# A 2 KB load as the first DMA of a row-maximum kernel, with the first 8 MB load behind the opening barrier

## The chip, the cores and the metric

The kernel runs on one core of a Trainium2 chip. The metric is the device time in microseconds (us); several runs give a median. A separate execution was recorded by the hardware profiler, and what is said below of the inside of a run comes from that one.

## The reference

For each of the 8192 rows of an fp32 matrix with 8192 columns, the largest absolute value:

```python
def reference(x):
    return np.linalg.norm(x, ord=np.inf, axis=1)
```

Every byte of the 268 MB input must be read once, and 8192 numbers are written.

## The kernel before

Each of the 128 SBUF partitions takes 64 rows: 38 "bulk" rows, 24 "tail" rows and 2 rows of the very first load. The first load (`x_f`, line 241) and the 19 bulk loads are of the same shape: 2 rows of 8192 values in each partition, 64 KB a partition and 8 MB in all. They go in turn into the three slots of one SBUF ring (lines 264 to 269). VectorE reduces each with one instruction, `absmax` (line 256), to two numbers per partition. The tail is 34 loads whose widths shrink toward the end (the table `TAIL`, loaded in line 303), so that little work is left when the last bytes land. Their reductions partly write a partial maximum into the ring just ahead of the next piece of the same row, so that the next reduction takes it in.

All loads are issued from SyncE (SP), in the order of the program, on one hardware DMA queue. A load into a used slot waits for the reduction that read the slot last. Loads rotate over eight completion semaphores, `DMAHW0` to `DMAHW7`; VectorE waits for the load's own semaphore. Two stores of results go out from ScalarE's queue near the end (lines 328 and 330), and a last one of 2 KB from SP (line 332).

Four edits are made on the finished instruction lists. What matters here:

- `start_first_load_early` (line 32) takes the first DMA that SP issues and puts it ahead of everything that SP does in the opening block. That block holds a barrier: each of SP, ScalarE and TensorE signals GpSimd, GpSimd answers with a release, and only then does an engine go on to the body. So the first DMA is issued before the barrier, and all others come behind it. In the code above the change, the first DMA is the 8 MB load of `x_f`.
- `finish_on_pool` (line 71) makes GpSimd wait for the last stores and clear the semaphores. The semaphore of the last store is left out of the clearing, since it is awaited last; what lies below it and above it is cleared by one instruction each, if there is anything there (lines 108 to 110).
- `drop_implied_waits` (line 132) removes waits that other waits imply. `open_without_vector` (line 184) takes VectorE out of the opening barrier.

`SPARE` unused semaphores are allocated ahead of the others (line 243), which sets the numbers that the others get. A tile `gap` rounds the small tiles to a multiple of 128 values, so that the ring starts at a fixed place (lines 250 to 253).

Of the kernel before, what the change touches and what calls it, by code (L numbers as in the profile page):

```python
# [12 lines left out]
F32 = mybir.dt.float32  # L13
# [4 lines left out]
HEAD, STEP = 32, 8  # L18
# [191 lines left out]
def kernel(  # L210
# [4 lines left out]
    B: int = 2,  # L215
    SLOTS: int = 3,
    PAD: int = 128,
    SPARE: int = 12,
):
    nc = tc.nc  # L220
    P = nc.NUM_PARTITIONS
# [11 lines left out]
    n_bulk_rows = rows // P - n_tail - B  # L233
# [7 lines left out]
    x_f = x_t[:, n_tail * cols :]  # L241
# [3 lines left out]
    pool = ctx.enter_context(tc.tile_pool(name="sbuf", bufs=1))  # L245
    r_bulk = pool.tile([P, n_bulk_rows], F32)
    n_soon = n_tail - 2
    r_soon = pool.tile([P, n_soon], F32)
    r_late = pool.tile([P, 2 + B], F32)
    used = [HEAD, n_bulk_rows, n_soon, 2 + B]  # L250
    gap = -sum(-(-n // STEP) * STEP for n in used) % PAD
    pool.tile([P, gap], F32, name="gap")
    ring = pool.tile([P, R], F32)
# [1 line left out]
    def absmax(o, i):  # L255
        return nc.vector.reduce_max(  # L256
            out=o, in_=i, axis=X, apply_absolute_value=True
        )

    def after(ins, first, kind):  # L260
        info = mybir.DependencyInfo(kind, mybir.DependencyReason.SCHED_ONLY)
        tc.add_manual_dep(ins.ins, first.ins.name, info, reason="order")

    for n in range(N):
        at = n % SLOTS * W
        t = ring[:, at : at + W]
        nc.sync.dma_start(out=t, in_=x_f if n == 0 else x_b[n - 1])
        r = r_late[:, 2:] if n == 0 else r_bulk[:, (n - 1) * B : n * B]
        absmax(r, t.rearrange("p (b c) -> p b c", b=B))
# [97 lines left out]
```

## Time and profile before

| | us |
|---|---|
| median of 3 runs | 626.26 (626.0 to 626.3) |
| the profiled execution's own time | 626.09 |
| its span, first to last instruction | 623.5 |
| VectorE busy | 552.3 (89% of the span) |
| bytes read from HBM | 268.44 MB, 431 GB/s over the span |

The span begins when SP issues the first DMA. The profiled execution's time is 2.6 us longer than its span: it also counts something ahead of the first instruction and, behind the last one shown, the landing of the last store. In the rows of the profile, `SPq` is SP's queue of instructions, among them the DMA issues. A DMA is issued by one instruction of some 0.3 us, is carried out by 16 DMA engines as packets of up to 64 KB, and lands later. In a table by windows the last two columns are the DMA share, which is the time of all packets that begin in the window as a share of 16 engines, and GB/s, which are their bytes. Both count a packet in the window in which it begins; so in a short window the share may be over 1, and the number of packets and their mean duration can be worked out.

### The profile page before, as it was taken

To read this page: it belongs to the slowest core of one execution; us is meant where nothing else is said; L and a number is where in the kernel's file an instruction comes from. 1 tells how busy PE (TensorE), PEld (TensorE's weight loads), DVE (VectorE), ACT (ScalarE), POOL (GpSimd) and SP (SyncE) were. 2 spreads that over 40 slices of the span, in tenths; PEclk is the share of its full clock that TensorE was granted. 3 is DMA by queue.
4 is the path that set the end of the run, shared out by engine and by line. 5 is a ranking of instruction groups with operands and counts; after the bars stand their busy time and mean duration, and the time that the engine had idled before them with its cause. 6 is when DMAs were issued, how large, how long until landed. Compare 5 with 4: busy or idle time off the path is not lost.

```text
span 623.5 us, 152 instructions
## 1 busy us (share of the span) xinstructions
DVE 552.3 (89%) x64; POOL 0.2 (0%) x4
## 2 busy tenths in 40 slices
DVE  0588988889988899888898888988889999999999
POOL 0000000000000000000000000000000000000000
DMA  9999999999999999999999999999999999999998
GB/s 404 471 404 446 429 408 467 404 471 404 471 404 467 408 441 433 408 467 404 471 404 471 404 467 408 441 433 408 467 428 435 415 437 419 447 422 431 428 425 357
DMA packets 8065, 268.48 MB, mean 431 GB/s; under 512 B 1152, under 2 KB 1152, under 8 KB 2560
## 3 DMA queue, kind: packets, MB, share of 16 engines
q1 hardware_dynamic: 7776, 268.44, 99.7%
q10 hardware_dynamic: 288, 0.03, 0.0%
q14 instruction: 1, 0.01, 0.0%
HBM read 268.44 MB, written 0.03 MB: 431 GB/s over the span
## 4 chain that ended last, share of the span: by engine, by line
DMA 65%; DVE 35%; another core or an unknown queue 0%; issue 0%; DVEq 0%
DMA ring<-in_x_dram 65%; DVE r_bulk L256 19%; DVE r_soon L256 14%; DVE ring L256 1%; DVEq L362 0%; DVE r_late L256 0%
## 5 line engine op out<-in xcount | busy, mean ns | idle before, releaser
L256 DVE TENSOR_REDUCE r_bulk<-ring 128x2 f32<-128x16384 f32 x19 | 327.2, 17220 | 40.0 <-DMA ring<-in_x_dram 40.0
L256 DVE TENSOR_REDUCE r_soon<-ring 128x1 f32<-128x8192 f32 (+9 forms) x18 | 148.0, 8249 | 8.4 <-DMA ring<-in_x_dram 8.4
L256 DVE TENSOR_REDUCE ring<-ring 128x1 f32<-128x4992 f32 (+23 forms) x24 | 59.7, 2539 | 0.1
L256 DVE TENSOR_REDUCE r_late<-ring 128x2 f32<-128x16384 f32 (+2 forms) x3 | 18.9, 6329 | 21.9 <-DMA ring<-in_x_dram 21.9
L351 POOL MEMSET const-bfloat16-1.0<- 128x1 bf16 x1 | 0.1, 101 | 0.0
L351 POOL MEMSET const-uint8-127<- 128x1 uint8 x1 | 0.1, 101 | 0.0
L351 POOL MEMSET const-float32-0.0<- 128x1 f32 x1 | 0.1, 98 | 0.2 <-issue 0.2
L351 POOL MEMSET const-float32-1.0<- 128x1 f32 x1 | 0.1, 98 | 0.0
## 6 DMA issues: line engine op xcount, KB each, us to landing
ring<-in_x_dram SPq DMA_DIRECT2D x3, 4096.0 KB, 30.7
ring<-in_x_dram SPq DMA_DIRECT2D x2, 3744.0 KB, 38.6
ring<-in_x_dram SPq DMA_DIRECT2D x1, 6592.0 KB, 37.0
ring<-in_x_dram SPq DMA_DIRECT2D x1, 5696.0 KB, 31.1
ring<-in_x_dram SPq DMA_DIRECT2D x1, 4480.0 KB, 37.5
ring<-in_x_dram SPq DMA_DIRECT2D x1, 3328.0 KB, 42.5
ring<-in_x_dram SPq DMA_DIRECT2D x1, 2912.0 KB, 40.8
ring<-in_x_dram SPq DMA_DIRECT2D x1, 2592.0 KB, 38.3
```

Source lines behind the costliest of these rows:

```text
L256: return nc.vector.reduce_max(out=o, in_=i, axis=X, apply_absolute_value=True)
L351: nc = _bacc.Bacc("TRN2", target_bir_lowering=False, num_devices=1)
```

## The change

A tile `opener` of 128 x 16 values is added. Ahead of the loop, SP issues a load of 16 values (64 bytes) into each fourth partition of it, from the first 64 bytes of the rows that the first 8 MB load brings for these partitions: 32 runs of 64 bytes, 2 KB. Nothing reads the tile. Since the load is now the first DMA that SP issues, `start_first_load_early` moves it, and no longer the 8 MB load, ahead of the barrier.

```diff
-    SPARE: int = 12,
+    SPARE: int = 11,
+    OPEN: int = 16,
...
+    opener = pool.tile([P, OPEN], F32)
-    used = [HEAD, n_bulk_rows, n_soon, 2 + B]
+    used = [HEAD, n_bulk_rows, n_soon, 2 + B, OPEN]
...
+    nc.sync.dma_start(out=opener[::4, :], in_=x_f[::4, :OPEN])
     for n in range(N):
         at = n % SLOTS * W
```

In the built program SP's list begins with the opener, then come the barrier and the 20 loads of 8 MB. The load of each place takes the semaphore of the next lane (the first 8 MB load `DMAHW1` in place of `DMAHW0`), so the eighth 8 MB load also waits for the lane that the opener used. The semaphore of the last store is no longer the lowest of its range, and GpSimd clears the range with two instructions in place of one. The order of the instructions of VectorE, ScalarE and TensorE is the same, and the ring starts at the same place: the opener's 16 values come out of `gap`.

## The prediction

> **What bounds the kernel now.** I read the page first, for what is busy, then tables by windows, for how evenly.
>
> ```profile
> span 623.5 us, 152 instructions
> ...
> DVE 552.3 (89%) x64; POOL 0.2 (0%) x4
> ...
> q1 hardware_dynamic: 7776, 268.44, 99.7%
> ```
>
> VectorE is idle for 11% of the span. The one queue of loads fills the 16 DMA engines for 99.7%. The next view asks whether there is a gap anywhere in the middle (window, its length, VectorE and GpSimd busy, clock, DMA share, GB/s):
>
> ```profile
> 5.00:105.00 100.00, 74.68 (x5) 0.00 (x0) 1.00 0.99 430
> 105.00:205.00 100.00, 89.51 (x6) 0.00 (x0) 1.00 1.01 440
> ...
> 505.00:605.00 100.00, 99.88 (x26) 0.00 (x0) 1.00 1.00 431
> 605.00:621.00 16.00, 16.00 (x11) 0.00 (x0) 1.00 1.01 419
> ```
>
> There is none: the share stays at 0.99 to 1.01 from 5 us until the last bytes. So every DMA engine runs packet behind packet, and it ends when it started in earnest plus a fixed amount of work. The time can move at only two places: how soon the engines run at full rate, and what follows the last landing. The change touches the first.
>
> For the first 5 us I read SP's own instructions (the first rows for the first load alone, the next for the barrier in SP's queue, then the second load), and then narrow windows.
>
> ```profile
> L267 SPq DMA_DIRECT2D ring<-in_x_dram x1: 362/362/362, 0.0 to 0.0; - x1
> ...
> DMA to landing us min/median/max: 21.8/21.8/21.8
> ```
> ```profile
> L351 SPq DRAIN  x1: 131/131/131, 0.4 to 0.4; - x1
> L351 SPq EVENT_SEMAPHORE  x1: 17/17/17, 0.7 to 0.7; - x1
> ```
> ```profile
> 0.77 0.80 SPq L267 DMA_DIRECT2D ring<-in_x_dram  x2
> ```
> ```profile
> 0.95:1.20 0.25, 0.00 (x0) 0.00 (x0) 1.00 10.50 3408
> 1.20:1.60 0.40, 0.00 (x0) 0.00 (x0) 1.00 0.00 0
> ```
> ```profile
> 1.60:1.65 0.05, 0.00 (x0) 0.00 (x0) 1.00 3.69 1311
> 1.65:1.75 0.10, 0.00 (x0) 0.00 (x0) 1.00 1.69 655
> ...
> 1.85:1.90 0.05, 0.00 (x0) 0.00 (x0) 1.00 3.03 1311
> 1.90:4.10 2.20, 0.00 (x0) 0.00 (x0) 1.00 0.00 0
> 4.10:4.60 0.50, 0.00 (x0) 0.00 (x0) 1.00 4.84 2097
> ```
> ```profile
> 4.56:4.60 0.04, 0.00 (x0) 0.00 (x0) 1.00 3.78 1638
> ```
>
> SP issues the first load at 0.00, passes the barrier at 0.7, and issues the second at 0.77. A packet of a big load is 65,536 bytes. In 0.95:1.20, 3408 GB/s x 0.25 us are 13 packets; their mean duration is 10.50 x 0.25 x 16 / 13 = 3.23 us. Three more engines begin late, one in each of the next three windows: durations 3.69 x 0.05 x 16 = 2.95, 1.69 x 0.10 x 16 = 2.70, and 3.03 x 0.05 x 16 = 2.42 us. Second packets: in 4.10:4.60 begin 16, of 4.84 x 0.50 x 16 / 16 = 2.42 us each. So 2.42 us is the full rate. The thirteen first packets carry 0.81 us of extra time, the late three 0.53, 0.28 and none. The later a packet begins, the less extra it has, and all 16 engines reach their second packet within 4.10 to 4.60. That looks like **one common stall at the start of all data**, which is over at about 4.10 - 2.42 = 1.7 to 4.60 - 2.42 = 2.2 us, and not like a price that each engine's first packet pays. The slowest engine begins its second packet in 4.56:4.60, say 4.58; a load counts as landed when its last engine is done, so this engine sets the pace.
>
> **The change part by part.**
>
> *The opener takes the first place.* SP issues a 2 KB load at 0.00 in place of 8 MB. No load of 2 KB is in this trace; the nearest row is the last store, of 2 KB from SP:
>
> ```profile
> 622.72 0.35 SPq L332 DMA_DIRECT2D out_dram<-r_late  x1
> ```
> ```profile
> 622.70:623.50 0.80, 0.00 (x0) 0.00 (x0) 1.00 0.00 0
> 623.50:623.56 0.06, 0.00 (x0) 0.00 (x0) 1.00 0.00 0
> 623.56:623.80 0.24, 0.00 (x0) 0.00 (x0) 1.00 0.32 9
> ```
> ```profile
> out_dram<-r_soon ACTq DMA_DIRECT2D x1, 11.0 KB, 2.1
> out_dram<-r_late SPq DMA_DIRECT2D x1, 2.0 KB, 1.4
> ```
>
> It costs SP 0.35 us against 0.36 for the load that it replaces, so SP's signal to the barrier and the release at 0.7 stay where they are. Its bytes are 32 runs of 64 bytes, two for each engine, against the 65,536 bytes of one packet: nothing.
>
> *The first 8 MB load moves behind the barrier.* It is issued at 0.77 in place of 0.00. Before, the first packets came 0.95 to 1.20 after the issue; the last store's came 623.56 - 622.72 = 0.84 after. I take the row of the load itself: 0.77 + 0.95 to 0.77 + 1.20 = 1.72 to 1.97. The loads behind it move too, the second from 0.77 to about 1.1; they only have to be in the queue before the first is through at some 21 us.
>
> *The stall.* Its price if it stays with the 8 MB load is the whole shift, +0.77. If it is over by time, because the opener has set the engines, the queue and the reads of the same rows going at 0.95 to 1.20, as the 8 MB load does now, then it has ended by 1.7 to 2.2, and the 8 MB load begins at 1.72 to 1.97 and finds it gone or nearly so. I take the second, from the late three: the packet that began at 1.85 ran at full rate, though it was the first of its engine and went to addresses that nothing had read. Then second packets begin at 1.97 + 2.42 = 4.39 at the latest, against 4.58: **-0.19 us**. With the store's 0.84 us from issue to packet it would be 0.77 + 0.84 + 2.42 = 4.03, or -0.55: the low end. What is late next is the DMA engines' own rate, which nothing here changes.
>
> The Trainium skill ("DMA: Bandwidth & Descriptors", Latency and other measured facts) gives some 800 ns as the least round trip to HBM for any transfer. By it the extra 0.81 us would be a round trip that each first packet pays, and the sum would be +0.77; the packet of 1.85:1.90, with no extra, speaks against it.
>
> *Waits, semaphores, the end.*
>
> ```profile
> SPq L267 <- DVE r_bulk L256: 303.7, 16, 19.1
> ```
> ```profile
> L303 SPq EVENT_SEMAPHORE  x3: 17/17/17, 560.5 to 599.9; - x3
> ```
> ```profile
> L362 POOLq EVENT_SEMAPHORE  x2: 17/17/17, 623.3 to 623.4; - x2
> ```
>
> The eighth 8 MB load gets a second wait, for the opener's lane, done long before; behind it in SP's queue stand the later loads. Such an extra wait takes 17 ns, and SP waits up to 19.1 us for VectorE there anyway, with a load still running in front of it: nothing. GpSimd clears semaphores with two instructions in place of one. A clear has no row; its own rows are 17 ns. GpSimd begins them at 623.4, and the last store lands at 622.72 + 1.4 = 624.1, for which it waits anyway: 0.7 us of cover. Without cover it would cost some 0.02 us. The opener's tile moves no other tile. The extra 2 KB of SBUF writes meet nothing at 1 us.
>
> **The sum** is -0.19 us: 626.09 - 0.19 = 625.90 against the profiled execution's own time. The median of the runs shown is 0.17 above that time, 626.26 - 0.19 = 626.07. I put the prediction between, at **626.0**.
>
> **The rivals.**
>
> *The stall is a price of the first packets of a big load* (or 64 bytes for each run are too little to end it; then the change does not do what it says). Then all moves by the 0.77 us of the later issue: 4.58 becomes 5.35, and 626.09 + 0.77 = 626.86; from the median 627.03. For it: thirteen of sixteen first packets carry the extra. Against it: the late three. It decides if first packets beginning at 1.72 to 1.97 still run about 3.2 us. This is the case on the other side.
>
> *The late three belong to each first big load.* The stall is gone, but three engines get their work up to 0.9 us later. The last begins at 0.77 + 1.90 = 2.67 and is done at 5.09: +0.51, 626.60. For it: nothing shows why they were late. Against it: packets of the last store all begin within 0.24 us.
>
> *The 8 MB load waits in the queue until the opener has landed*, 1.4 to 2.1 us after its issue by the two rows of stores, and then pays the stall: at worst 2.1 + 0.25 + 3.23 = 5.58, +1.00, 627.1. Over 0.2% only if the opener took more than 2.35 us. Against it: between loads on this queue there is no gap (share 0.99 to 1.01). The skill's page (Queues, rings and completion order) says that descriptors on one ring carry no barrier, which those windows agree with.
>
> **How the numbers follow.** 0.2% is 1.25 us, about what a measurement of this kernel can tell from no change. Chances: the forecast 0.55, the stall paid again 0.25, the late three 0.12, the queue held 0.05, something unseen 0.03. The first three are all within 1.25 us. Faster by more would need full rate at 2.16 - 1.25 = 0.91, 0.14 us after the load's issue, where 0.84 is the least seen. So faster 0.02, same 0.93, slower 0.05 (half of the queue held, and the unseen). The range goes from 625.5 (626.09 - 0.55) to 627.0, where the stall paid again ends by both bases within 0.03; about 0.15 is left out.
>
> **What would show it.** In the profile of the changed kernel: the 8 MB load's issue at 0.7 to 0.8; its first packets at 1.7 to 2.0, each 2.42 us long; all second packets begun by 4.4; and everything from the first reduction on 0.2 us earlier. First packets of 3.2 us mean the first rival, packets begun after 2.3 the second, all first packets after 2.0 the third. If second packets begin earlier and the time does not follow, the argument that each engine runs without a gap is wrong.

## The result

The changed kernel takes 627.30 us (median of 22 runs, 627.16 to 627.74), the kernel before 626.13 (22 runs, 626.00 to 626.44). The ratio is 1.0019, with a 95% interval of 1.0013 to 1.0025: slower by 1.17 us, and no run of one kernel reaches the times of the other. A gain of 0.2 had been forecast, to 626.0.

SP's part of the first 1.5 us in the changed kernel: the opener's issue, then the barrier in SP's queue, then the first 8 MB load (start, duration, instruction).

```profile
L266 SPq DMA_DIRECT2D opener<-in_x_dram x1: 547/547/547, 0.0 to 0.0; - x1
```
```profile
L354 SPq DRAIN  x1: 367/367/367, 0.6 to 0.6; - x1
L354 SPq EVENT_SEMAPHORE  x1: 17/17/17, 1.1 to 1.1; - x1
```
```profile
1.19 0.35 SPq L270 DMA_DIRECT2D ring<-in_x_dram  x1
```

The opener's issue took 0.55 us where 0.35 had been assumed, and the drain behind it (the instruction by which SP reports to the barrier) 0.37 where it took 0.13 before. So SP was let through the barrier at 1.1 and not at 0.7, and the first 8 MB load was issued at 1.19 and not at 0.77.

The DMA in narrow windows of the changed kernel (window, length, VectorE and GpSimd, clock, DMA share, GB/s):

```profile
1.25:1.65 0.40, 0.00 (x0) 0.00 (x0) 1.00 0.07 5
2.10:2.50 0.40, 0.00 (x0) 0.00 (x0) 1.00 6.52 2130
2.65:2.70 0.05, 0.00 (x0) 0.00 (x0) 1.00 3.93 1311
2.95:3.00 0.05, 0.00 (x0) 0.00 (x0) 1.00 3.04 1311
3.20:3.25 0.05, 0.00 (x0) 0.00 (x0) 1.00 3.02 1311
```
```profile
5.20:5.85 0.65, 0.00 (x0) 0.00 (x0) 1.00 3.72 1613
...
5.00:105.00 100.00, 73.40 (x5) 0.00 (x0) 1.00 1.02 440
505.00:605.00 100.00, 99.89 (x26) 0.00 (x0) 1.00 1.00 431
```

The opener's packets are in the first row and over by 1.65. The 8 MB load then starts just as it did before, only later: thirteen packets of 6.52 x 0.40 x 16 / 13 = 3.21 us, then three late ones of 3.14, 2.43 and 2.42. First packets of 3.2 us are the sign that the prediction named for its first rival. All second packets begin within 5.20 to 5.85, against 4.10 to 4.60 before. From there on nothing differs; the engines run without a gap. The reductions into `r_late`, which hold the first and the last of the kernel (changed kernel, then the kernel before):

```profile
L258 DVE TENSOR_REDUCE r_late<-ring x3: 817/951/17220, 23.1 to 623.2; 128x2 f32<-128x16384 f32 x1, 128x1 f32<-128x773 f32 x1, 128x1 f32<-128x646 f32 x1
```
```profile
L256 DVE TENSOR_REDUCE r_late<-ring x3: 817/949/17220, 21.9 to 621.9; 128x2 f32<-128x16384 f32 x1, 128x1 f32<-128x773 f32 x1, 128x1 f32<-128x646 f32 x1
```

The first reduction starts 1.2 to 1.3 us later and so does the last. All of the loss lies ahead of the first landing.

### The profile page after: what moved, and what is told of

It reads as the page before. It is cut to its first block, busy times and chain, and to the rows that moved or that the text cites. A ratio compares the mean times of both kernels' runs of the same rounds, so it can differ in the third digit from the quotient of the medians.

```text
span 624.8 us, 154 instructions
## 1 busy us (share of the span) xinstructions
DVE 552.4 (88%) x64; POOL 0.2 (0%) x4
## 4 chain that ended last, share of the span: by engine, by line
DMA 59%; DVE 40%; another core or an unknown queue 0%; issue 0%; DVEq 0%; SPq 0%
DMA ring<-in_x_dram 59%; DVE r_bulk L258 19%; DVE r_soon L258 11%; DVE ring L258 9%; DVEq L365 0%; SPq L270 0%; SPq L306 0%; DVE r_late L258 0%
```

## The experiments

Two questions follow. Does an opener take anything off the start of the 8 MB load, or does the time just move with that load's issue? And why did the issue of a 2 KB load hold up SP? The theory to test: the time moves one to one with the issue of the first load that brings bulk data, whatever small load stands in front. The rival: an opener does help, and what it gains is lost again at the barrier.

### The opener's shape: e1_all, e3_consec, e9_step_sbuf, e10_step_hbm

```diff
-    nc.sync.dma_start(out=opener[::4, :], in_=x_f[::4, :OPEN])
+    nc.sync.dma_start(out=opener[:, :],   in_=x_f[:, :OPEN])     # e1_all
+    nc.sync.dma_start(out=opener[:32, :], in_=x_f[:32, :OPEN])   # e3_consec
+    nc.sync.dma_start(out=opener[::4, :], in_=x_f[:32, :OPEN])   # e9_step_sbuf
+    nc.sync.dma_start(out=opener[:32, :], in_=x_f[::4, :OPEN])   # e10_step_hbm
```

> The opener reads 64 bytes for each of the 128 partitions in place of each fourth. Theory (the time moves with the issue of the first 8 MB load, and what delayed that issue beyond 0.77 us is the shape of the opener, 32 rows): opener issue 0.35 us, SP's drain 0.13 us, 8 MB load issued at 0.77, first packets of 3.2 us, time 0.77 above the kernel before, about 626.9. Rival (any load of 64-byte runs delays SP so): issue 0.55 us, drain 0.37, 8 MB load at 1.19, time 1.2 above, about 627.3.

> The opener reads 64 bytes for partitions 0 to 31 in place of each fourth of 128. Theory 1 (it is the number of rows, 32, that makes the opener slow to issue): issue 0.55 us, drain 0.37, 8 MB load at 1.19, time 1.2 above the kernel before. Theory 2 (it is the step of four partitions): issue 0.35, drain 0.13, 8 MB load at 0.77, time 0.77 above.

> The changed kernel's opener with the step of four partitions on the SBUF side alone (it reads the rows of partitions 0 to 31). Theory S (the step in SBUF makes the issue slow): opener issue 0.55 us, drain 0.37, 8 MB load at 1.19, time near 627.3. Theory H (the step in the source rows does): 0.37, 0.13, 0.78, time near 626.95.

> The changed kernel's opener with the step of four on the source rows alone (it writes partitions 0 to 31). Theory S (the step in SBUF makes the issue slow): opener issue 0.37 us, drain 0.13, 8 MB load at 0.78, time near 626.95. Theory H (the step in the source rows does): 0.55, 0.37, 1.19, time near 627.3.

The opener's issue and SP's drain in the four, in this order:

```profile
L266 SPq DMA_DIRECT2D opener<-in_x_dram x1: 361/361/361, 0.0 to 0.0; - x1
...
L354 SPq DRAIN  x1: 131/131/131, 0.4 to 0.4; - x1
```
```profile
L266 SPq DMA_DIRECT2D opener<-in_x_dram x1: 370/370/370, 0.0 to 0.0; - x1
...
L354 SPq DRAIN  x1: 126/126/126, 0.4 to 0.4; - x1
```
```profile
L266 SPq DMA_DIRECT2D opener<-in_x_dram x1: 543/543/543, 0.0 to 0.0; - x1
...
L354 SPq DRAIN  x1: 367/367/367, 0.6 to 0.6; - x1
```
```profile
L266 SPq DMA_DIRECT2D opener<-in_x_dram x1: 383/383/383, 0.0 to 0.0; - x1
...
L354 SPq DRAIN  x1: 126/126/126, 0.4 to 0.4; - x1
```

Only the step over SBUF partitions makes the issue and the drain slow. The number of runs does not (128 or 32), nor does the step in the source rows. With the cheap shapes the 8 MB load is issued at 0.77 to 0.79, and e1_all takes 626.93, e3_consec 626.95 and e10_step_hbm 626.94 us (one run); with the step in SBUF alone e9_step_sbuf takes 627.33 (one run), as the changed kernel does. So 0.4 of the 1.17 us is the opener's step in SBUF.

### No opener at all: e2_none

```diff
-    nc.at_finalize(start_first_load_early)
```

> No opener, and no DMA ahead of the barrier: the first 8 MB load is the first DMA, behind the barrier. Theory (an opener buys nothing, the stall is paid by the 8 MB load anyway): with nothing of SP's to wait for, the barrier is released by GpSimd at about 0.58, the load issued at about 0.7 after the same starting point, time 0.6 to 0.7 above the kernel before, about 626.8, and 0.5 below the changed kernel. Rival (the opener takes part of the start's price off the 8 MB load, and loses more through the late barrier): more than 0.77 above, 627.0 or more.

The 8 MB load's issue in this kernel:

```profile
0.73 0.38 SPq L267 DMA_DIRECT2D ring<-in_x_dram  x1
```

626.95 us is 0.79 above the kernel before: 0.1 more than the theory gave, and by the number alone at the lower edge of what the rival gave. What decides is the comparison with the two cheap openers, 626.93 and 626.95, of which the load stands 0.04 to 0.05 us further back. By these medians an opener of 64 bytes for each run takes 0.06 us off the start at most. The recorded intervals of the three ratios (1.0004 to 1.0022) are too wide to show so little, so the second packets have to say it. All 16 of e2_none begin in this window:

```profile
4.70:5.45 0.75, 0.00 (x0) 0.00 (x0) 1.00 3.23 1398
```

That is 3.97 to 4.72 us after the load's issue. In e3_consec they begin at 4.85 to 5.40, which is 4.07 to 4.62 after it, and in the kernel before 4.10 to 4.60. Of the rival at most some 0.1 us is left.

### Opener and 8 MB load both ahead of the barrier: e12_both

`start_first_load_early` moves the first two DMAs of SP, the opener of e3_consec and the 8 MB load.

```diff
-                first.instructions = head[:at] + [moved] + head[at:]
+    first.instructions = head[:at] + moved + head[at:]     # moved: the first two
```

> The opener of e3 (partitions 0 to 31) and the first 8 MB load are both ahead of the barrier, the opener first. Theory (a load flows at full rate only 1.6 to 2.3 us after its own issue, and the time of the kernel moves one to one with the issue of the first load that brings bulk data): 8 MB load issued at 0.40 to 0.45, time 0.40 to 0.45 above the kernel before, 626.55 to 626.6. Rival 1 (what costs in the openers of 64 bytes is the barrier in front of the 8 MB load): time of the kernel before. Rival 2 (an opener shortens the lag if the load follows closely): below 0.3 above.

```profile
0.44 0.41 SPq L272 DMA_DIRECT2D ring<-in_x_dram  x1
```

```profile
4.40:5.25 0.85, 0.00 (x0) 0.00 (x0) 1.00 2.85 1234
```

626.64 us, against 626.09 for the kernel before in the same session: 0.55 more, 0.1 above the upper end of what the theory gave. The recorded interval of the ratio, 0.9999 to 1.0017, is too wide to exclude the rivals (no change, or below 0.3). But the eleven runs lie at 626.49 to 626.80 and the fifteen of the kernel before at 625.97 to 626.21, and the second packets, in the window above, begin 3.96 to 4.81 us after the load's issue, on both sides of the 4.10 to 4.60 of the kernel before. So within 0.1 us neither the barrier nor the distance between the two loads matters beyond when the 8 MB load is issued. All points together, with the difference to the median of the kernel before in the same session:

| kernel | 8 MB load issued at | median, us | above before, us |
|---|---|---|---|
| before | 0.00 | 626.09 to 626.16 | |
| e12_both | 0.44 | 626.64 | 0.55 |
| e2_none | 0.73 | 626.95 | 0.79 |
| e1_all | 0.77 | 626.93 | 0.77 |
| e3_consec | 0.78 | 626.95 | 0.79 |
| e10_step_hbm (1 run) | 0.79 | 626.94 | 0.85 |
| changed kernel | 1.19 | 627.30 | 1.17 |
| e9_step_sbuf (1 run) | 1.19 | 627.33 | 1.24 |

The line from issue to time holds within 0.11 us. In e2_none the issue is counted from SP's drain, the first instruction there.

### Does every restart pay? e6_slots1

```diff
-    SLOTS: int = 3,
+    SLOTS: int = 1,
```

> The kernel before with one ring slot in place of three: each load waits for the reduction before it, so each finds the DMA engines idle for some 17 us. Only the first packets are looked at, not the time. Theory A (each restart of idle engines pays the price): first packets of every load mostly 3.0 to 3.5 us long, all second packets 3.3 to 3.9 after the first begin, issue to landing near 21.8 us for every 8 MB load. Theory B (the price is paid only at the program's beginning): first packets 2.42 from the second load on, landing some 21.0 us after the issue.

The second load of this kernel and one of the middle, each with its issue. In the windows the first row has the 16 first packets, the second row the 16 second ones:

```profile
39.03 0.33 SPq L267 DMA_DIRECT2D ring<-in_x_dram  x1
```
```profile
390.52 0.33 SPq L267 DMA_DIRECT2D ring<-in_x_dram  x1
```
```profile
39.95:40.85 0.90, 0.00 (x0) 0.00 (x0) 1.00 3.55 1165
43.10:43.60 0.50, 0.00 (x0) 0.00 (x0) 1.00 4.84 2097
391.45:392.55 1.10, 0.00 (x0) 0.00 (x0) 1.00 2.80 953
394.50:395.15 0.65, 0.00 (x0) 0.00 (x0) 1.00 3.72 1613
```
```profile
DMA to landing us min/median/max: 21.6/21.8/22.0
```

The first packets last 3.55 x 0.90 = 3.2 and 2.80 x 1.10 = 3.1 us in the mean, and second packets begin 4.1 to 4.6 and 4.0 to 4.6 us after the issue, with late starters among the first. That is the start of the program over again, in the middle of the kernel, on a queue and engines that have long been in use; all twenty 8 MB loads land 21.6 to 22.0 us after their issue. Nothing at the program's beginning is special, so there is nothing that an opener could set going once and for all. Theory A holds; only the second packets come 3.05 to 3.7 us after the first begin, a little sooner than it gave.

### A larger, useful opener: e4_split2048, e7_split_tail, e8_tail_only, e5_split512_tail

```diff
-        nc.sync.dma_start(out=t, in_=x_f if n == 0 else x_b[n - 1])
+        if n == 0:
+            nc.sync.dma_start(out=t[:, :OPEN], in_=x_f[:, :OPEN])   # OPEN 2048 or 512
+            nc.sync.dma_start(out=t[:, OPEN:], in_=x_f[:, OPEN:])
+        else:
+            nc.sync.dma_start(out=t, in_=x_b[n - 1])
```

> No opener. The first 8 MB load is split: the first 2048 of the 16384 values of each partition (1 MB, 2.4 us of all 16 engines) ahead of the barrier, the other 14336 behind it; the same bytes in all, and the first reduction waits for both. Theory (the start's price is paid by a load that finds the engines without data; a load queued before the engines run dry does not pay it): 1 MB issued at 0.00, its first packets carry the extra, the second load at 0.77 follows without a gap and its packets run at the full rate, time within 0.2 of the kernel before. Rival (the first packet of every load issued behind the barrier is slow, or the late barrier itself costs): 0.6 us or more above.

The second part's issue, its first packets, VectorE's waits, and for comparison VectorE's waits in the kernel before:

```profile
0.77 0.33 SPq L270 DMA_DIRECT2D ring<-in_x_dram  x1
```
```profile
4.17:4.56 0.39, 0.00 (x0) 0.00 (x0) 1.00 5.55 2395
```
```profile
DVE r_bulk L257 <- DMA ring<-in_x_dram: 39.8, 19, 2.1
DVE r_late L257 <- DMA ring<-in_x_dram: 21.9, 1, 21.9
DVE r_soon L257 <- DMA ring<-in_x_dram: 8.4, 4, 2.1
DVE ring L257 <- DMA ring<-in_x_dram: 0.8, 1, 0.8
```
```profile
DVE r_bulk L256 <- DMA ring<-in_x_dram: 40.0, 19, 2.2
DVE r_late L256 <- DMA ring<-in_x_dram: 21.9, 1, 21.9
DVE r_soon L256 <- DMA ring<-in_x_dram: 8.4, 4, 2.1
```

The window holds 2395 GB/s x 0.39 us = 934 KB: the sixteen first packets of the second part (57,344 bytes each) and two last ones of the first (8 KB, 0.3 us). That leaves (5.55 x 0.39 x 16 - 0.6) / 16 = 2.12 us for each, the full rate. The second part was queued 3.4 us ahead of its turn and pays nothing; the first reduction waits 21.9 us, as before the change. So far the theory. But the time is 626.70, 0.54 above the kernel before, and the `ring` row shows where: one wait of 0.8 us in the tail, which the kernel before hasn't got. At that place (DMA of 592.30 to 592.35) stands

```profile
q14 instruction: 1, 0.01, 38.6%
```

a fetch of 8 KB of instructions (0.386 x 0.05 us x 16 = 0.31 us of one DMA engine), among the loads of the tail. The kernel before has one such fetch too, but at 621.4 us, when the loads are all but over. From the fetch on, one of the 16 engines signals its share of each tail load 0.7 to 0.9 us behind all others, where in the loads before it the last was 0.03 us behind. That is more than the 0.31 us of the fetch; where the rest comes from is not shown. The split gives VectorE's first reduction a second wait, an instruction of its own, the 71st of VectorE's list in the built program (the trace shows 69 of them, and 68 of the 70 in the kernel before). So two neighbouring tail widths were changed, which saves one instruction, and the same widths put alone into the kernel before:

```diff
-    (114688, 8960), (123648, 7488), ...
+    (114688, 8192), (122880, 8256), ...
```

> The split of e4 (1 MB of the first load ahead of the barrier, the other 7 MB behind it), with two neighbouring tail widths changed from 8960 and 7488 to 8192 and 8256, which leaves VectorE 70 instructions, as before the change, where e4 has 71. Theory (the loss of e4 came from the 8 KB instruction fetch at 592.3 us on one DMA engine, brought on by VectorE's 71st instruction; the start itself cost nothing): no fetch before the last load, first reduction to last 0.0 to 0.2 earlier than before, time 625.9 to 626.2. Rival (the fetch is not tied to VectorE's count, or the split costs elsewhere): fetch again near 592, time near 626.7.

> The kernel before with the two tail widths of e7 alone; VectorE has 69 instructions. It is the control for e7: both theories expect the time of the kernel before within 0.2 (625.9 to 626.4); what it differs by is the widths' own share in e7.

> As e7, with only the first 512 values of each partition (256 KB, 0.6 us of all engines) ahead of the barrier. Theory (the start's price of some 0.8 us per engine is paid once by the first bulk data, and a load queued before these are through follows for free): the small load runs from 1.0 to 0.8 + 0.6 later, 2.4, the second load's packets are there at 1.75 to 2.0, so no gap; time as e7 within 0.1. Rival (the price is paid again by the first 64 KB packets unless the engines already run at the full rate when these arrive, as the openers of 64 bytes suggest): up to 0.8 above, 626.2 to 626.9.

e7_split_tail takes 626.04 us, e8_tail_only 626.05, the kernel before 626.15 in the same session (ratio 0.9998 for both, 0.9989 to 1.0008 and 0.9988 to 1.0007: not to be told from the kernel before). e7 has no fetch among the loads (it comes at 621.6), and the wait is gone. A split that brings 1 MB ahead of the barrier thus costs nothing that these runs can tell, and gains nothing beside its control: no version here beats the kernel before by more than its interval.

e5_split512_tail takes 626.36, 0.3 above e7, which has the same tail, and 0.2 above the kernel before (ratio 1.0005, 0.9996 to 1.0014: by itself not to be told from it). The theory as it was put, e7 within 0.1, missed; the rival's range, 626.2 to 626.9, has the time in it. Its second part is issued at 0.77 too, and the 16 second packets of that part (63,488 bytes, 2.34 us at full rate) begin in

```profile
4.70:5.30 0.60, 0.00 (x0) 0.00 (x0) 1.00 3.90 1693
```

So full rate begins at 4.70 - 2.34 to 5.30 - 2.34, that is 1.6 to 2.2 us after this part's own issue, though the engines were already moving the first part: the price is paid again in part, as the rival said (first packets of 2.8 us in the mean, against 2.34). The same reckoning, second packets less 2.42 us less the issue, gives 1.7 to 2.2 in the kernel before, 1.6 to 2.2 in the changed one, and 1.7 to 2.2 and 1.6 to 2.2 for the two loads of e6. **Each big load here has a lag of its own of about 2 us from issue to full rate; the lag is hidden when the load is queued far enough ahead of its turn.** In e4 3.4 us ahead was enough; between that and e5 nothing was tried. In e5 the engines had 16 KB each to do, 0.6 us, while the second part came 0.77 later: by this account 0.77 - 0.6 = 0.17 us are lost. The medians say 0.2 to 0.3, which agrees, but the runs alone could not show a loss so small.

### Is the fetch a matter of VectorE's instructions? e11_dve71

```diff
-    pool.tile([P, gap], F32, name="gap")
+    spot = pool.tile([P, gap], F32, name="gap")
...
+    nc.vector.memset(spot[:, :], 0.0)
     nc.sync.dma_start(out=out_t[:, n_soon:], in_=r_late[:])
```

> The kernel before with one small VectorE instruction added (it sets the unused gap tile), so that VectorE has 71 instructions as in e4; no split, no opener. Theory (the 71st instruction of VectorE brings the 8 KB instruction fetch into the loads): a fetch before the last load, one DMA engine late by some 0.9 us from there on, time 626.6 to 627.1. Rival (the fetch of e4 has to do with its split load): fetch only after the loads, at about 621.4, time 626.1 to 626.4.

One run, 626.86 us. VectorE's wait in the tail, and the DMA queues of the stretch 580 to 600 us:

```profile
DVE ring L256 <- DMA ring<-in_x_dram: 0.5, 1, 0.5
```
```profile
q1 hardware_dynamic: 713, 8.51, 99.7%
q14 instruction: 1, 0.01, 0.1%
```

The fetch is back at 592.8 us, without split or opener: one more instruction in VectorE's list is enough to move it from the end of the loads to some 29 us ahead of it. With 69 instructions (e8) and 70 (before, e7) the one fetch comes at 621.4 to 621.6. In e6_slots1, whose trace shows 74 VectorE instructions, it comes at 1141.6, 12 us before the loads are over. Why the place goes by the length of the list, no run shows.

## Why the prediction was wrong

- **The frame held.** The engines run without a gap from their second packets to the last byte, so the time is the start plus a constant. First reduction and last moved by the same 1.2 to 1.3 us.
- **The step that failed: the stall "is over by time", set off by the opener.** The late three, with less extra time the later they began, were read as one stall that ends at a point of time, and the point was counted from the program's first DMA. It does end at a point of time, but counted from the load's own issue: about 1.6 to 2.2 us behind it, whether the issue is at 0.00, at 1.19, or at 390.52. A 2 KB load ahead does not start that clock for the 8 MB load. With the data at hand the two readings could not be told apart, since the only load that found the engines idle was also the first; 0.55 against 0.25 was too sure. So the 8 MB load paid the stall again, and the term that the prediction had at -0.19 is the whole shift of 0.77, as the first rival had it; the cheap openers measure 0.77 and 0.79.
- **The term that was mis-sized: the opener's issue.** It was taken from the last store's row, 0.35 us, with the release of the barrier unmoved. That store goes over the SBUF partitions one by one; the opener writes each fourth. Measured: 0.55 for the issue and 0.37 for the drain, by which the barrier opened 0.4 later. 0.77 and 0.4 make up the 1.17. The first rival, 626.86 to 627.03, was short by this, and the range ended at 627.0 because it left no room for a slower issue.
- **The late three** are there again (three of the first packets in the changed kernel, others in e6). As a rival they were worth 0.51 more; they are a part of the lag, not a cost beside it.
- **The queue held until the opener lands** did not happen: the 8 MB load's first packets come 2.10 - 1.19 = 0.9 us after its issue, as before the change. In e1_all they begin at 1.73, and the opener lands at 1.8.
- **Waits, semaphores and the end** cost nothing, as forecast: from the start of the last reduction to the end of the span it is 1.6 us in both kernels, and both times are 2.6 us longer than their spans.
- **The rule of the Trainium skill** ("DMA: Bandwidth & Descriptors", Latency and other measured facts) was set aside for a reason that does not hold. That page of the Trainium skill gives some 800 ns as the least round trip to HBM. The two loads of e6, which find the engines idle, have first packets 0.7 to 0.8 us longer than the full rate (3.1 to 3.2 against 2.42), and the sum that the prediction drew from the rule, +0.77, is what the cheap openers measure. By the account above the packet of 1.85:1.90 had no extra because it began late in its load's lag. That the extra time is such a round trip, no run shows: in e4 the first packets of a load that was queued early have none of it.

What stays open is what the 2 us consist of: packets show as begun 1 us after the issue and reach full rate only at about 2, and no run here looked inside. Nor was it tried whether three particular engines are the late ones. And e9_step_sbuf, e10_step_hbm, e11_dve71 and e6_slots1 are single runs.

## What to carry to other kernels

When the DMA engines are full from beginning to end, the issue time of the first load that brings bulk data goes into the total one to one; put that load itself first, or a useful part of it that keeps the engines busy for as long as the next load is delayed (here 1 MB did, and 256 KB fell 0.17 us short by the estimate above). A tiny load ahead of it saved no more than some 0.1 us here: price it as plain delay, and take the price of its issue from a row with the same access pattern on the SBUF side. After any edit that adds an instruction to a long list, look whether an instruction fetch has moved into the loads.

## What the runs showed that was not expected

- A load of 32 runs of 64 bytes with a step of four partitions in SBUF takes 0.55 us to issue and 0.37 us to drain; without the step 0.37 and 0.13 (e9 against e3).
- A load of 8 MB, or of nearly that, reaches full rate some 1.6 to 2.2 us after its own issue: at the beginning, after 17 us of idle engines, and behind another load that is too short to cover it.
- One more VectorE instruction, the 71st, moved an 8 KB instruction fetch from 621 us, the end of the loads, to about 592 us in two kernels (e4, e11). VectorE waited 0.8 and 0.5 us once, and the kernels came out 0.5 and 0.8 us slower (the second in one run).
